# One hybrid decoder layer in fp32 on one core: two weight sums instead of three as side work, two sums formed in the second up phase, and the side work spread otherwise

## The chip, the cores and the metric

The kernel runs on one core of one Trainium2 chip. The metric is the device time of one execution in microseconds. The core's engines each run their own queue in order: TensorE (PE, with its weight loads PEld), VectorE (DVE), ScalarE (ACT), GpSimd (POOL) and SyncE (SP), which computes nothing and issues most DMAs. An instruction waits on semaphores of other engines or of DMAs; what is behind it in its queue waits with it.

## The reference

One decoder layer for 512 prompt tokens and 8 x 4 sample tokens, 544 columns in all. What matters here:

```python
z = rmsnorm(h, g) @ w_in            # pooling input, queries, six k/v sets, gates
A = pool_mixer(pool_in);  B = native_sparse_attention(q, kv)
h = h + rmsnorm((sig(ga) * (A @ w_pool_proj) + sig(gb) * (B @ w_nsa_proj)) @ w_out)
up = rmsnorm(h) @ w_up              # 2048 -> 2 * 5632, columns: val | gate
val, gate = split(up)
y = (gelu(causal_conv(gate)) * val) @ w_down
h = h + rmsnorm(y)
```

## The kernel before

Activations lie transposed: 128 channels on the partitions, 544 tokens along the free side, in two halves of 272. Every product in full fp32 accuracy is made of three: the high part of the weights by the high part of the activations, high by low, and low by high (L404 to L406). So each weight block is loaded raw and split.

**Units of weights.** `plan()` lists 1220 units in the order of use, most of four blocks of 128x128 (`UB`). The class `Weights` carries each through three steps. `load` issues the DMA into a raw tile `wr` (SP). `split` part 0 makes the high part `wh` on ScalarE (L247), part 1 the low part `wl` on VectorE (L249, raw minus high). `get` hands the unit to TensorE. `progress` is called between the matmuls of a unit: at a quarter and a half of it, it splits the unit that is `ahead` units further and issues a load beyond it. Raw tiles and parts come from rings of buffers that `grow` lengthens: three raw tiles in the opening, eight in the up phases.

**The up product.** It is a Winograd form of Strassen's scheme over halves of the contraction (k) and of the columns (val and gate) and the two token halves. For a column block j there are weight quarters 0 (gate, first k half), 1 (gate, second), 2 (val, first), 3 (val, second). The first up phase does quarters 0 and 1 with the first token half. The second up phase has per j five products, in this order: `t1` with weights s1 = q2 + q3, `t2` with s2 = s1 - q0, `b22` with s4 = q1 - s2, `t3` with s3 = q0 - q2, `t4` with q3. Two units make a product, ten units a column; 44 columns. `b22` adds into the bank of `t1` and `t3` into the bank of `t2`, so ScalarE's copy of `t1` (L1489, val) and VectorE's add from `t2` (L1491, sl) have to be done before. The conv of the column before (L1430 to L1441) runs beside it, in pieces that `later` issues.

**Side work.** s1, s2 and s3 are not known beforehand. `sum_stage` forms them during the input projections: for each of 88 pieces (j and half of k) it loads quarters 0, 2, 3 (`su`, 768 KB), does three VectorE operations in place (L367, L369, L371) and writes three sums back to DRAM (`sums_d`, 768 KB). The up phase loads them from there. s4 is formed when its unit is split: L246 subtracts the raw tile of s2, two units older, ahead of the cast. The su ring has three tiles, so the load of piece n + 2 waits for the write of piece n - 1.

**Order.** All of it is written out in one program order. `tick` is called between matmuls; it runs `later` calls that are due and steps two generators, `bg` (attention stages, residual chains, preparation) and `side` (the sums), each at a `rate`: a rate of 0.5 is a step for every second tick. `wait(n)` is n empty steps. The rates are set by hand at the stages (L1073 on). `h1_chain` (L1286 on) is the residual and norm chain of a token half; its squares are added up by GpSimd (L1309) and a matmul `nrh` (L428) sums them over the partitions.

In the opening, tokens arrive tile by tile (`x`, L475), ScalarE makes the high part (L479), VectorE the low (L480), ScalarE squares; units 0 to 15 each belong to one tile. There `ahead` is 1, from unit 14 on it is 2.

Of the kernel before, what the change touches and what calls it, by code (L numbers as in the profile page):

```python
# [12 lines left out]
F32 = mybir.dt.float32  # L13
# [3 lines left out]
OP = mybir.AluOpType  # L17
# [4 lines left out]
P = 128  # L22
# [12 lines left out]
FT = DFF // P  # L35
# [5 lines left out]
KH = KT // 2  # L41
UB = 4
UW = UB * P
# [60 lines left out]
def quad(j, q):  # L104


    if isinstance(q, str):
        b = [(q, k, j) for k in range(KH)]
    else:
        b = [("up", q % 2 * KH + k, (FT if q < 2 else 0) + j) for k in range(KH)]  # L110
    return [tuple(b[c:c + UB]) for c in range(0, KH, UB)]


SLOT = {"s2": 0, "s3": 1, "s1": 2}


def offsets(units):
# [61 lines left out]
class Weights:  # L179


    def __init__(self, nc, dram, sums, units):
        self.nc, self.dram, self.sums, self.units = nc, dram, sums, units
        self.i = self.nd = self.ns = 0
        self.raw, self.done = {}, {}
        self.rings = {"wraw": [], "wpart": []}
        self.turn = {"wraw": 0, "wpart": 0}
        self.ahead, self.raws = 1, 2
        self.off, _ = offsets(units)
        self.kept, self.again = {}, {}  # L190

# [16 lines left out]
    def load(self, n):  # L208
        while self.nd < min(n, len(self.units)):
            if self.nd in self.again:  # L210
                self.nd += 1
                continue
            i = self.nd
            pool, n_ = self.slot("wraw")
            t = self.raw[i] = pool.tile([P, UW], F32, name=f"wr{i}", tag="wraw", bufs=n_)
            b, w = self.units[i][0], self.width(i)
            mat, k, j = b[0]
            if mat in SLOT:
                src = self.sums[j, k // UB][:, SLOT[mat], :]
            else:  # L220
                o, n, q = self.off[quad(j, 1)[k // UB] if mat == "s4" else b]
                src = self.dram[o:o + n * P * w].rearrange("(p q c) -> p q c", q=n, c=w)[:, q, :]
            self.nc.sync.dma_start(t[:, :w], src)
            self.nd += 1

    def split(self, i, part):

        if i in self.again:
            if part == 0:
                self.done[i] = self.kept[self.again[i]]  # L230
            else:
                self.ns = i + 1
            return
        if part == 0:
            self.load(i + 1)
            if i in self.kept:
                self.done[i] = self.kept[i]
            else:
                pool, n = self.slot("wpart")
                self.done[i] = tuple(pool.tile([P, UW], F32R, name=f"w{p}{i}", tag="w" + p, bufs=n) for p in "hl")  # L240
        hi, lo = self.done[i]
        c = slice(0, self.width(i))
        raw = self.raw[i]
        if part == 0:
            if self.units[i][0][0][0] == "s4":
                self.nc.vector.tensor_tensor(raw, raw, self.raw[i - 2], OP.subtract)  # L246
            self.nc.scalar.copy(hi[:, c], raw[:, c])  # L247
        else:
            self.nc.vector.tensor_tensor(lo[:, c], raw[:, c], hi.bitcast(F32)[:, c], OP.subtract)  # L249
            self.raw.pop(i - 2, None)  # L250
            self.ns = i + 1

    def finish(self, i):
        while self.ns <= i:
# [25 lines left out]
def layer(ctx: ExitStack, tc: tile.TileContext, a: dict):  # L280
    nc = tc.nc
# [17 lines left out]
    dr, dr_es = pool("scratch", space=DRAM)  # L299
    psp, ps_es = pool("ps", space=PSUM)  # L300

    sums_d = dr.tile([FT, KH // UB, P, 3, UW], F32, name="sums_d")
    sup, su_es = pool("sums", "right")
    ws = Weights(nc, a["wst"], sums_d, plan())
    ws.grow(wp, 3, 3)
# [44 lines left out]
    def sum_stage():  # L350

        pieces = [(j, c) for j in range(FT) for c in range(KH // UB)]
        tiles = {}

        def load(n):
            j, c = pieces[n]
            t = tiles[n] = sup.tile([P, 3, UW], F32, name=f"su{j}_{c}", tag="su", bufs=3)
            o = ws.off[quad(j, 0)[c]][0]
            nc.sync.dma_start(t, a["wst"][o:o + 3 * P * UW].rearrange("(p q c) -> p q c", q=3, c=UW))

        load(0)
        load(1)
        yield from wait(10)
        for n, (j, c) in enumerate(pieces):
            t = tiles.pop(n)
            a11, a21, a22 = [t[:, q, :] for q in range(3)]
            V.tensor_tensor(a22, a21, a22, OP.add)  # L367
            yield
            V.tensor_tensor(a21, a11, a21, OP.subtract)  # L369
            yield  # L370
            V.tensor_tensor(a11, a22, a11, OP.subtract)  # L371
            yield from wait(2)
            if n + 2 < len(pieces):
                load(n + 2)
            yield from wait(4)
            nc.sync.dma_start(sums_d[j, c], t)
            yield from wait(2)

    def wait(n):
        for _ in range(n):  # L380
            yield
# [129 lines left out]
    for k in range(0, KT, 2):  # L511
        if k + 2 < KT:
            load_x(k + 2)
            load_x(k + 3)
        ws.load(k + 4)
        if k == 8:
            load_consts()
        if k == 0:
            ws.finish(0)
            split_x(1)  # L520
            square_x(0)
            square_x(1)
        if k + 2 < KT:
            split_x(k + 2)
            split_x(k + 3)
            square_x(k + 2)
            square_x(k + 3)
        if k == KT - 2:
            ws.ahead, ws.raws = 2, 3
            ws.finish(k + 2)  # L530
            for h in range(2):
                later(4 * h, lambda h=h: norm_factor([acc[:, HS[h]]], r1[:, HS[h]], f"nra{h}", (tmpn, tmps)))
            tick(0)
        for _ in range(2):
            unit(lambda mat, m: psA[m], U, lambda k: k == 0, lambda k: k == KT - 1, byk=True)
# [539 lines left out]
    def background():  # L1075
        yield from compress_stage()
        yield from natural_stage()
        t1_es.close()
        side["rate"] = 0.55
        yield from sample_stage()  # L1080
        s2_es.close()
        side["rate"] = 0.8
        yield from prompt_stage()

    bg["gen"] = background()
    bg["rate"] = 0.7
    side["gen"], side["rate"] = sum_stage(), 0.77

    first_evac()
    for m in range(3, 21):  # L1090
# [190 lines left out]
    def h1_chain(h):  # L1281

        sl = HS[h]
        xr, sq = {}, {}

        def load(k):  # L1286
            xr[k] = hp_.tile([P, H2], F32, name=f"xr{h}_{k}", tag="xr", bufs=4)
            nc.sync.dma_start(xr[k], a["xT"][:, k, sl])

        for k in range(3):  # L1290
            load(k)
        yield from wait(4)
        norm_factor([acc2[:, sl]], rm[:, sl], f"nrm{h}")
        yield
        for k in range(KT + 2):
            if k < KT:
                if k + 3 < KT:
                    load(k + 3)
                t = mo[:, k, sl]
                V.scalar_tensor_tensor(t, t, gains[:, 1, k:k + 1], rm[:, sl], OP.mult, OP.mult)  # L1300
                V.tensor_tensor(t, t, xr.pop(k), OP.add)
            if 1 <= k <= KT:
                j = k - 1
                t = mo[:, j, sl]
                sq[j] = acc3[:, sl] if j == 0 else hp_.tile([P, H2], F32, name=f"sqh{h}_{j}", tag="sqh", bufs=3)
                S.activation(sq[j], t, AF.Square)
                nc.sync.dma_start(h1_d[:, j, sl], t)
            if k > 2:
                G.tensor_tensor(acc3[:, sl], acc3[:, sl], sq.pop(k - 2), OP.add)  # L1309
            yield  # L1310
        yield from wait(5)
        norm_factor([acc3[:, sl]], r2[:, sl], f"nrh{h}")
        yield
        for k in range(KT + 1):
            if k < KT:
                t = mo[:, k, sl]
                V.scalar_tensor_tensor(t, t, gains[:, 2, k:k + 1], r2[:, sl], OP.mult, OP.mult)
            if h == 0:
                if k < KT:
                    S.copy(vh0[:, k, :], t)  # L1320
                if k:
                    V.tensor_tensor(vl0[:, k - 1, :], mo[:, k - 1, sl], vh0.bitcast(F32)[:, k - 1, :], OP.subtract)
            yield
# [48 lines left out]
    for h in range(2):  # L1372
        for m in range(KT - NSPLIT, KT):
            ps = bank(f"wo{m}_{h}", m, h)
            full("out", m, ps, MX, lambda m, h: mo_evac(m, ps, h))
        if h == 0:
            bg["gen"], bg["rate"], bg["credit"] = h1_chain(0), 0.85, 1.0
    drain()
    mg_es.close()
    w2p, w2_es = pool("weights2", "left")  # L1380
# [26 lines left out]
                    nc.sync.dma_start(stash_d[j + i], st[i])  # L1407
    drain()
    v0_es.close()
    gw, gw_es = pool("gate", "right")  # L1410
    cw, ch, co = ffn["cw"], ffn["ch"], ffn["co"]
    ge, stash = {}, {}
# [138 lines left out]
    for ci, (c0, c1) in enumerate(CHUNKS):  # L1551
# [21 lines left out]
        for n in range(ws.ahead, KT):  # L1573
            i = ws.i + n
# [29 lines left out]
    ad_es.close()  # L1604
    y_es.close()
    w2_es.close()
    w1_es.close()
    ps_es.close()
    dr_es.close()
# [94 lines left out]
```

## Time and profile before

| | |
|---|---|
| median of 3 runs | 3075.03 us (3069.4 to 3075.3) |
| profiled execution | 3070.8 us, span 3068.9 us, granted clock 0.98 |
| PE busy | 2914.3 us, 95% |
| DVE busy | 1888.4 us, 62% |
| ACT busy | 1149.4 us, 37% |
| moved by DMA | 593.04 MB, mean 193 GB/s |
| sum pieces loaded / written | 88 x 768 KB, 5.3 us to landing / 88 x 768 KB, 6.0 us |

The stages, by the trace: opening to about 62 us, input projections with the attention stages beside them to 956, pooling projection and mixer to 1124, the two projections and merge to 1322, output projection to 1538, first up phase to 1800, second to 2489, down product to the end. A busy PE is not PE at its peak, as matmuls are pipelined; idle time in front of an instruction and what ended it tell more. In a time line the start is in us from the span's start.

### The profile page before, as it was taken

Reading aid. Unit: us, or ns where it says so; the run is one execution under the profiler, and the core shown is the slowest. Engines: PE = TensorE matmul, PEld = TensorE weight load, DVE = VectorE, ACT = ScalarE, POOL = GpSimd, SP = SyncE. Lnnn points to the kernel's source line nnn. Section 1 sums busy time; section 2 is a strip of 40 time slices with the busy share of each in tenths; the row PEclk is TensorE's granted clock in tenths of the full one; section 3 lists DMA queues with packets and bytes.
Section 4 is the critical chain, followed back from the end, with each engine's and each line's share of the span. In section 5 each row is a group of like instructions: output and inputs, shape, how many; then the busy total and the mean of one; then the engine's idle time right before and its main releaser. Section 6 shows DMA issues by size and latency. Waiting matters only on the chain. (4 is left out here: it accounts for less than half of the span.)

```text
span 3068.9 us, 59917 instructions
## 1 busy us (share of the span) xinstructions
PE 2914.3 (95%) x22799; PEld 2805.6 (91%) x22799; DVE 1888.4 (62%) x3706; ACT 1149.4 (37%) x2390; POOL 258.1 (8%) x400
## 2 busy tenths in 40 slices
PE   7798898999999899999899999999999999999995
PEld 7788876899999799999899999999999999999995
DVE  5334443688886566644887557777777764444457
ACT  4111122444443132223456555555455453222223
POOL 3222221000000210001220000000000000000004
PEclk9899999999999999999999999999999999999998
DMA  4966677644555788844686666666666663333343
GB/s 152 249 226 231 226 262 268 218 156 164 180 182 180 197 260 294 293 128 122 179 277 218 229 218 205 206 204 202 203 204 205 212 203 114 111 110 109 100 130 105
DMA packets 304111, 593.04 MB, mean 193 GB/s; under 512 B 52811, under 2 KB 93164, under 8 KB 303822
## 3 DMA queue, kind: packets, MB, share of 16 engines
q1 hardware_dynamic: 280040, 557.74, 56.0%
q10 hardware_dynamic: 16614, 14.68, 2.1%
q0 software_dynamic: 7168, 16.79, 1.7%
q8 instruction: 179, 2.93, 0.4%
q14 instruction: 110, 0.90, 0.1%
HBM read 461.77 MB, written 127.31 MB: 192 GB/s over the span
## 5 line engine op out<-in xcount | busy, mean ns | idle before, releaser
L249 DVE TENSOR_TENSOR wl<-wr,wh 128x512 fp32r<-128x512 f32 (+1 forms) x1198 | 839.2, 707 | 782.8 <-ACT wh L247 671.7
L247 ACT CAST wh<-wr 128x512 fp32r<-128x512 f32 (+1 forms) x1198 | 726.8, 618 | 1278.7 <-PE dn L405 324.5
L404 PE MATMUL in<-uh,wh 128*128 128x272 f32 x1600 | 496.5, 310 | 42.2 <-DVE gz L1101 16.2
L406 PE MATMUL in<-uh,wl 128*128 128x272 f32 x1600 | 465.7, 291 | 2.5 <-DVE wl L249 2.5
L405 PE MATMUL in<-ul,wh 128*128 128x272 f32 x1600 | 465.6, 291 | 0.0
L404 PEld LDWEIGHTS in<-uh,wh 128*128 128x128 f32 x1600 | 305.8, 191 | 86.1 <-issue 73.7
L404 PE MATMUL dn<-h,wh 128*128 128x272 f32 x1320 | 380.6, 288 | 1.8 <-DVE y L1582 1.8
L406 PE MATMUL dn<-h,wl 128*128 128x272 f32 x1320 | 382.1, 289 | 0.0
L405 PE MATMUL dn<-l,wh 128*128 128x272 f32 x1320 | 379.7, 288 | 0.0
L406 PEld LDWEIGHTS in<-uh,wl 128*128 128x128 f32 x1600 | 305.6, 191 | 3.2 <-DVE wl L249 3.2
L405 PEld LDWEIGHTS in<-ul,wh 128*128 128x128 f32 x1600 | 306.8, 192 | 0.7
L404 PEld LDWEIGHTS dn<-h,wh 128*128 128x128 f32 x1320 | 249.0, 189 | 2.4 <-issue 2.4
L405 PEld LDWEIGHTS dn<-l,wh 128*128 128x128 f32 x1320 | 248.9, 189 | 0.0
L406 PEld LDWEIGHTS dn<-h,wl 128*128 128x128 f32 x1320 | 248.3, 188 | 0.0
L404 PE MATMUL p<-vh,wh 128*128 128x272 f32 x704 | 204.2, 290 | 0.1
L405 PE MATMUL p<-vl,wh 128*128 128x272 f32 x704 | 203.9, 290 | 0.0
L406 PE MATMUL p<-vh,wl 128*128 128x272 f32 x704 | 203.3, 289 | 0.0
L406 PE MATMUL wo<-mh,wl 128*128 128x272 f32 x512 | 150.9, 295 | 4.9 <-DVE wl L249 4.9
L404 PE MATMUL wo<-mh,wh 128*128 128x272 f32 x512 | 150.5, 294 | 2.0 <-ACT wh L247 1.9
L405 PE MATMUL wo<-ml,wh 128*128 128x272 f32 x512 | 149.2, 291 | 0.0
L404 PEld LDWEIGHTS p<-vh,wh 128*128 128x128 f32 x704 | 132.7, 188 | 0.4 <-ACT st L1405 0.3
L406 PEld LDWEIGHTS p<-vh,wl 128*128 128x128 f32 x704 | 132.5, 188 | 0.2 <-DVE wl L249 0.2
(353 smaller groups left out, 6854.6 us busy)
## 6 DMA issues: line engine op xcount, KB each, us to landing
wr<-wst SPq DMA_DIRECT2D x929, 256.0 KB, 3.4
su<-wst SPq DMA_DIRECT2D x88, 768.0 KB, 5.3
sums_d<-su SPq DMA_DIRECT2D x88, 768.0 KB, 6.0
wr<-sums_d SPq DMA_DIRECT2D x264, 256.0 KB, 3.1
stash_d<-st SPq DMA_DIRECT2D x44, 272.0 KB, 2.1
act_d<-val SPq DMA_DIRECT2D x44, 272.0 KB, 2.1
ar<-act_d SPq DMA_DIRECT2D x44, 272.0 KB, 3.0
sg_d<-gz SPq DMA_DIRECT2D x32, 272.0 KB, 2.1
```

The source lines that it names most:

```text
L247: self.nc.scalar.copy(hi[:, c], raw[:, c])
L249: self.nc.vector.tensor_tensor(lo[:, c], raw[:, c], hi.bitcast(F32)[:, c], OP.subtract)
L404: T.matmul(ps, wh, xh, start=first(k), stop=False, skip_group_check=skip)
L405: T.matmul(ps, wh, xl, start=False, stop=False, skip_group_check=skip)
L406: T.matmul(ps, wl, xh, start=False, stop=last(k), skip_group_check=skip)
```

## The change

- s3 is no longer formed as side work. `sum_stage` does two VectorE operations (s1, s2) and writes 512 KB a piece; it still loads three quarters. s3 is formed as q3 - s2 in the second up phase, from a plain load of quarter 3 and the raw tile of s2, four units older.
- Both subtracts (s4 and s3) move: `combine` issues them behind the low part of the unit before, not in front of the own cast. Two more raw buffers (`weights3`) hold the older tiles.
- The side work's rates: 0.35, 0.3, 0.85 and then 1.1, before 0.77, 0.55, 0.8.
- In the opening, units are split two ahead from the start, unit 1 before the loop.
- `h1_chain` waits 10 steps, not 5, ahead of its second norm; for the first half its rate is 1.0, not 0.85.

```diff
-SLOT = {"s2": 0, "s3": 1, "s1": 2}
+SLOT = {"s2": 0, "s1": 1}
+PLAIN = {"s4": 1, "s3": 3}
...
-        self.ahead, self.raws = 1, 2
+        self.ahead, self.raws = 2, 3
...
         if part == 0:
-            if self.units[i][0][0][0] == "s4":
-                self.nc.vector.tensor_tensor(raw, raw, self.raw[i - 2], OP.subtract)
             self.nc.scalar.copy(hi[:, c], raw[:, c])
         else:
             self.nc.vector.tensor_tensor(lo[:, c], raw[:, c], hi.bitcast(F32)[:, c], OP.subtract)
-            self.raw.pop(i - 2, None)
+            self.raw.pop(i - 4, None)
             self.ns = i + 1
+            self.combine(i + 1)
+
+    def combine(self, i):
+
+        mat = self.units[i][0][0][0] if i < len(self.units) else None
+        if mat in PLAIN:
+            self.nc.vector.tensor_tensor(self.raw[i], self.raw[i], self.raw[i - (2 if mat == "s4" else 4)], OP.subtract)
...
-        yield from wait(10)
+        yield from wait(12)
...
-            V.tensor_tensor(a22, a21, a22, OP.add)
-            yield
-            V.tensor_tensor(a21, a11, a21, OP.subtract)
-            yield
-            V.tensor_tensor(a11, a22, a11, OP.subtract)
+            V.tensor_tensor(a21, a21, a22, OP.add)
+            yield
+            V.tensor_tensor(a11, a21, a11, OP.subtract)
+            yield
...
-            nc.sync.dma_start(sums_d[j, c], t)
+            nc.sync.dma_start(sums_d[j, c], t[:, :2, :])
...
             ws.finish(0)
             split_x(1)
+            ws.finish(1)
...
-        side["rate"] = 0.55
+        side["rate"] = 0.3
...
-        side["rate"] = 0.8
+        side["rate"] = 0.85
         yield from prompt_stage()
+        side["rate"] = 1.1
...
-    side["gen"], side["rate"] = sum_stage(), 0.77
+    side["gen"], side["rate"] = sum_stage(), 0.35
...
-        yield from wait(5)
+        yield from wait(10)
         norm_factor([acc3[:, sl]], r2[:, sl], f"nrh{h}")
...
-            bg["gen"], bg["rate"], bg["credit"] = h1_chain(0), 0.85, 1.0
+            bg["gen"], bg["rate"], bg["credit"] = h1_chain(0), 1.0, 1.0
...
+    w3p, w3_es = pool("weights3", "right")
+    ws.grow(w3p, 2, 0)
```

**VectorE in the second up phase**, from column 30 into column 31 (units 898 to 907 are column 31; `wl903<-wr903,wh903` is the low part of unit 903, `cv30` the conv of column 30, `sl31` the add that reads the bank of `t2`). Before:

```order
L1503 TENSOR_TENSOR val30_28743<-sl30_28695,utr30_28742 128x272
L246 TENSOR_TENSOR wr903_28838<-wr903_28838,wr901_28798 128x512
L249 TENSOR_TENSOR wl903_28957<-wr903_28838,wh903_28956 128x512
L1435 SCALAR_TENSOR_TENSOR cv30_28948<-ge30_28697,cw_21334,cv30_28948 128x560
L1436 SCALAR_TENSOR_TENSOR cv30_28948<-ge30_28697,cw_21334,cv30_28948 128x560
L249 TENSOR_TENSOR wl904_28982<-wr904_28856,wh904_28981 128x512
L249 TENSOR_TENSOR wl905_29001<-wr905_28876,wh905_29000 128x512
L1440 TENSOR_TENSOR val30_28743<-val30_28743,cv30_28948 128x512
L1441 TENSOR_TENSOR val30_28743<-val30_28743,cv30_28948 128x32
L249 TENSOR_TENSOR wl906_29022<-wr906_28894,wh906_29021 128x512
L1491 TENSOR_TENSOR sl31_28904<-sl31_28904,ug31_28949 128x272
```

Now, from the same operation on (the subtract of unit 903 stands one row above the first):

```order
L1511 TENSOR_TENSOR val30_28719<-sl30_28670,utr30_28718 128x272
L248 TENSOR_TENSOR wl903_28935<-wr903_28815,wh903_28934 128x512
L257 TENSOR_TENSOR wr904_28833<-wr904_28833,wr900_28756 128x512
L1443 SCALAR_TENSOR_TENSOR cv30_28926<-ge30_28672,cw_21365,cv30_28926 128x560
L1444 SCALAR_TENSOR_TENSOR cv30_28926<-ge30_28672,cw_21365,cv30_28926 128x560
L248 TENSOR_TENSOR wl904_28960<-wr904_28833,wh904_28959 128x512
L257 TENSOR_TENSOR wr905_28853<-wr905_28853,wr901_28775 128x512
L248 TENSOR_TENSOR wl905_28980<-wr905_28853,wh905_28979 128x512
L1448 TENSOR_TENSOR val30_28719<-val30_28719,cv30_28926 128x512
L1449 TENSOR_TENSOR val30_28719<-val30_28719,cv30_28926 128x32
L248 TENSOR_TENSOR wl906_29001<-wr906_28871,wh906_29000 128x512
L1499 TENSOR_TENSOR sl31_28881<-sl31_28881,ug31_28927 128x272
```

The s4 subtract of unit 903 went above the add into val30, and the two s3 subtracts (units 904 and 905) stand ahead of the conv and between the low parts of 904 and 905. ScalarE's order there is the same as before; its cast of 905 now has that subtract in front of it.

**SP after the opening**, from the first sum pieces on (`su0_0` is the load of a piece, `wr20` that of unit 20). Before:

```order
L359 DMA su0_0_1046<-wst 128x1536
L359 DMA su0_1_1048<-wst 128x1536
L223 DMA wr20_1054<-wst 128x512
L548 DMA kvT<-cz_114 128x544 x3
L223 DMA wr21_1087<-wst 128x512
L223 DMA wr22_1117<-wst 128x512
L223 DMA wr23_1147<-wst 128x512
L223 DMA wr24_1184<-wst 128x512
L359 DMA su1_0_1195<-wst 128x1536
L548 DMA kvT<-cz_114 128x544
L223 DMA wr25_1217<-wst 128x512
L376 DMA sums_d_71<-su0_0_1046 128x1536
```

Now:

```order
L224 DMA wr20_1050<-wst 128x512
L365 DMA su0_0_1058<-wst 128x1536
L365 DMA su0_1_1060<-wst 128x1536
L553 DMA kvT<-cz_114 128x544 x3
L224 DMA wr21_1087<-wst 128x512
L224 DMA wr22_1117<-wst 128x512
L224 DMA wr23_1147<-wst 128x512
L224 DMA wr24_1181<-wst 128x512
L553 DMA kvT<-cz_114 128x544
L224 DMA wr25_1212<-wst 128x512
L224 DMA wr26_1249<-wst 128x512
L224 DMA wr27_1280<-wst 128x512
```

The third piece load and the first write-back have left this place; they come behind units 31 and 34.

**SP in the two projections** (units 286 to 292). Before:

```order
L223 DMA wr286_15114<-wst 128x512
L223 DMA wr287_15146<-wst 128x512
L359 DMA su40_1_15174<-wst 128x1536
L223 DMA wr288_15183<-wst 128x512
L223 DMA wr289_15213<-wst 128x512
L376 DMA sums_d_71<-su39_1_14945 128x1536
L223 DMA wr290_15256<-wst 128x512
L359 DMA su41_0_15284<-wst 128x1536
L223 DMA wr291_15290<-wst 128x512
L223 DMA wr292_15324<-wst 128x512
```

Now:

```order
L224 DMA wr286_15007<-wst 128x512
L365 DMA su37_1_15018<-wst 128x1536
L224 DMA wr287_15039<-wst 128x512
L381 DMA sums_d_71<-su36_1_14858 128x1024
L224 DMA wr288_15075<-wst 128x512
L365 DMA su38_0_15093<-wst 128x1536
L224 DMA wr289_15108<-wst 128x512
L381 DMA sums_d_71<-su37_0_14936 128x1024
L224 DMA wr290_15150<-wst 128x512
L365 DMA su38_1_15178<-wst 128x1536
L224 DMA wr291_15184<-wst 128x512
L381 DMA sums_d_71<-su37_1_15018 128x1024
```

A piece now stands to every two units here, before to every three. In SP's order up to the load of unit 134 (four ahead of unit 130) there are 16 piece loads and 14 write-backs, before 32 and 30; from there to that of unit 212, 27 and 26, before 25 and 25; behind it 45 and 48, before 31 and 33. Both finish ahead of the output projection.

In the opening, the loads of `x4` and `x5` stand behind those of units 4 and 5; before they stood ahead of unit 4. The low part of unit 1 stands ahead of the low parts of `x2` and `x3` on VectorE, before behind them.

## Rows read from the trace of the kernel before

**Rows 1.** Busy time by stage: start:end, length, engines (instructions), clock, DMA share, GB/s.

```profile
62.00:135.00 73.00, 52.72 (x373) 50.34 (x371) 29.40 (x53) 10.98 (x18) 16.92 (x34) 0.86 0.87 230
135.00:570.00 435.00, 396.47 (x3169) 348.34 (x3169) 181.46 (x478) 88.11 (x183) 94.56 (x172) 0.96 0.72 243
956.00:1124.00 168.00, 150.18 (x1113) 144.91 (x1112) 90.10 (x166) 38.61 (x69) 31.30 (x28) 0.95 0.73 206
1124.00:1322.00 198.00, 194.78 (x1535) 193.74 (x1534) 130.14 (x228) 55.13 (x95) 0.00 (x0) 0.99 0.83 285
1830.00:2440.00 610.00, 602.17 (x4693) 593.43 (x4693) 468.44 (x861) 306.07 (x627) 3.89 (x39) 1.00 0.63 205
...
1140.00:1150.00 10.00, 10.00 (x82) 10.00 (x81) 9.01 (x18) 3.07 (x5) 0.00 (x0) 1.00 0.92 335
```

**Rows 2.** Waits of PE over the span: releaser, us in total, times, longest.

```profile
PE cps L666 <- DMA X<-cache: 17.7, 3, 7.8
PE in L404 <- DVE gz L1101: 16.2, 7, 7.2
PE in L404 <- DVE kz L555: 15.6, 1, 15.6
PE st L404 <- ACT wh L247: 11.2, 6, 2.7
PE uqk L404 <- ACT val L1489: 10.7, 43, 2.4
PE po L404 <- ACT wh L247: 9.2, 4, 4.1
...
PE nrh L428 <- POOL acc L1309: 4.6, 1, 4.6
```

**Rows 3.** Waits of SP's queue from 62 to 570.

```profile
SPq L359 <- DMA sums_d<-su: 35.8, 10, 11.6
```

**Rows 4.** Waits of SP's queue from 956 to 1322.

```profile
SPq L359 <- DMA sums_d<-su: 62.2, 18, 6.6
```

**Rows 5.** Time line of DVE, one column: start, duration, operation [idle before, releaser].

```profile
2148.20 0.44 DVE L1498 TENSOR_TENSOR sl<-sl,ug 128x272 f32<-128x272 f32 x1 [0.29 <-PE ug L406]
...
2151.08 0.69 DVE L249 TENSOR_TENSOR wl<-wr,wh 128x512 fp32r<-128x512 f32 x1 [0.76 <-PE utr L405]
...
2152.03 0.69 DVE L246 TENSOR_TENSOR wr<-wr,wr 128x512 f32<-128x512 f32 x1
...
2154.24 0.81 DVE L1435 SCALAR_TENSOR_TENSOR cv<-ge,cw,cv 128x560 f32<-128x560 f32 x1
...
2157.13 1.50 DVE L249 TENSOR_TENSOR wl<-wr,wh 128x512 fp32r<-128x512 f32 x2 [1.25 <-PE ug L405]
2158.55 0.69 DVE L1440 TENSOR_TENSOR val<-val,cv 128x512 f32<-128x512 f32 x1
...
2159.25 0.69 DVE L249 TENSOR_TENSOR wl<-wr,wh 128x512 fp32r<-128x512 f32 x1
2159.85 0.43 DVE L1491 TENSOR_TENSOR sl<-sl,ug 128x272 f32<-128x272 f32 x1
...
2163.79 0.44 DVE L1498 TENSOR_TENSOR sl<-sl,ug 128x272 f32<-128x272 f32 x1 [0.29 <-PE ug L406]
```

**Rows 6.** Time line of ACT, the same column.

```profile
2152.83 0.62 ACT L247 CAST wh<-wr 128x512 fp32r<-128x512 f32 x1 [1.78 <-DVE wr L246]
2153.36 0.85 ACT L1430 ACTIVATE cv<-ge,cw 128x560 f32<-128x560 f32 x1
...
2156.50 0.60 ACT L247 CAST wh<-wr 128x512 fp32r<-128x512 f32 x1
2157.01 0.38 ACT L1489 COPY val<-uqk 128x272 f32<-128x272 f32 x1
2157.28 1.66 ACT L247 CAST wh<-wr 128x512 fp32r<-128x512 f32 x3
```

**Rows 7.** Time line of PE, the same column.

```profile
2157.44 0.39 PE L404 MATMUL uqk<-b22h,wh 128*128 128x272 f32 x1 [0.20 <-ACT val L1489]
...
2160.57 0.29 PE L404 MATMUL ug<-t3h,wh 128*128 128x272 f32 x1
```

More of the change, by code (lines that the diff above doesn't have):

```diff
@@ L220, in load @@
             else:
-                o, n, q = self.off[quad(j, 1)[k // UB] if mat == "s4" else b]
+                o, n, q = self.off[quad(j, PLAIN[mat])[k // UB] if mat in PLAIN else b]
                 src = self.dram[o:o + n * P * w].rearrange("(p q c) -> p q c", q=n, c=w)[:, q, :]
@@ L300, in layer @@
     psp, ps_es = pool("ps", space=PSUM)
-    sums_d = dr.tile([FT, KH // UB, P, 3, UW], F32, name="sums_d")
+    sums_d = dr.tile([FT, KH // UB, P, 2, UW], F32, name="sums_d")
     sup, su_es = pool("sums", "right")
@@ L528, in layer @@
         if k == KT - 2:
-            ws.ahead, ws.raws = 2, 3
             ws.finish(k + 2)
@@ L1606, in layer @@
     w2_es.close()
+    w3_es.close()
     w1_es.close()
```

## The prediction

> **What bounds the kernel now.** I read the stages first, then who TensorE waits for, then one column of the stage that the new subtract goes into. TensorE is the bound: it is busy 602.2 of 610 us in the steady part of the second up phase [rows 1]. Its losses lie early: 20.3 us idle in the 73 us from 62 to 135, 38.5 us in the 435 us up to 570, 17.8 us in the pool stage from 956 to 1124 [rows 1]. By cause, the largest waits are 17.7 us for the page loads of the compression, 16.2 us behind VectorE in the gate evacuations, 15.6 us once in the kv evacuation, and 11.2 us for weight casts in the opening [rows 2]. The single wait of 15.6 us belongs to the sum work: SP, whose queue carries every weight load, stood up to 11.6 us at the load of a sum piece until an older piece was written back [rows 3].
>
> In the second up phase nothing looks late in that list except 10.7 us (43 waits) for the copy of val [rows 2]. The reader is to see there that one column's VectorE and ScalarE work is a single chain. It begins when the t3 product ends (L1498 at 2148.20) and it returns 15.59 us later (2163.79) [rows 5]. Two of its links hold TensorE: the copy of val (2157.01, ends 2157.39) frees the b22 product at 2157.44, and L1491 (2159.85, ends 2160.28) reads the bank that the t3 product adds to from 2160.57 [rows 5 to 7]. The second has only 0.29 us to spare.
>
> **The change, part by part.** *The third weight sum in the second up phase.* One VectorE subtract of 128x512 leaves each of the 88 sum pieces; 88 new ones stand in the second up phase, two a column, and every subtract there (L257) stands behind the low part of the unit before. I follow the column of rows 5 to 7 in the new order, with these steps of the old: a subtract's start to its cast's start 0.80 us (2152.03 to 2152.83); a cast's start to its low part's start 0.63 (2156.50 to 2157.13); VectorE's spacing of two such operations 0.60 (2159.25 to 2159.85).
> The low part of the first s4 unit starts at 2151.08 as before. The second s4 subtract follows it at 2151.68 (it stood at 2152.03). Its cast comes at 2152.48, the conv's first step on ScalarE 0.53 us later at 2153.01 and, lasting 0.85, ready at 2153.86. But VectorE now does the low part at 2153.11 and the new s3 subtract at 2153.71, so L1435's successor starts at 2154.31, against 2154.24. The gain of 0.35 us is eaten, and the val copy is 0.07 us later.
> From there: the next cast at 2156.57, its low part at 2157.20, the second s3 subtract at 2157.80, and only then its cast, at 2158.60; that low part at 2159.23 (before: 2157.91, from a cast at 2157.28 that waited for no subtract); L1440's successor at 2159.83, the next low part 0.70 us later at 2160.53, L1491's successor at 2161.13, ended after 0.43 at 2161.56. TensorE may start t3 some 0.05 us after that, at 2161.61 instead of 2160.57: 1.04 us late. A restart costs about 0.1 more (the first matmul behind the val wait took 0.39 against 0.29 [rows 7]). A column has no slack to win this back, since the chain starts again from the end of t3. 44 columns x 1.15 us = 51 us. Bounds: nothing, if the bank's reader were not waited for, and 60 us, if each of the two subtracts delayed the whole column by 0.69. I take +51, since the same steps explain the old column: from its cast at 2157.28 they put L1491 at 2159.81, where it is at 2159.85 [rows 5, 6].
>
> The row of that stage shows VectorE busy 468.4 of 610 us, 77% [rows 1]; two more subtracts of 0.69 us in 15.59 make 86%, still under TensorE. The Trainium skill (Perfetto Trace Analysis, Identifying the Most-Contended Engine) judges VectorE's headroom by just this occupancy. By it the subtracts would cost nothing and the sum would be 51 us lower, as in the first rival; the trace here agrees that VectorE has room, and not that the room lies where the column could use it.
>
> *The sum work thinned early.* By the order, the part up to unit 130 (to 570 us) keeps 16 piece loads of 32 and 14 write-backs of 30, and a write-back is 512 KB instead of 768. Of the 16.8 MB moved from 62 to 135 (230 GB/s) some 4.7 MB leave, three loads and three writes of 0.79. No load of a piece stands in SP's way there any more, so the 11.6 us go, while the rest of the traffic, that kept the DMA engines 87% busy, stays. Bounds 0 and -16; I take -10. The waits for the page loads: 32 loads a group are issued one after another and the last one's landing is waited for; less traffic shortens landings, not the number of issues. Bounds 0 and -18; I take half, -9. The gate waits (16.2): SP is held there by the sample's own loads and stores as well; bounds 0 and -16, I take -8. The clock returns some with each: 0.86 granted from 62 to 135 and 0.96 to 570 [rows 1]; that is at most another 10 us, which I leave to the range.
>
> *The sum work packed later.* From unit 208 to the drain 45 loads stand where 31 stood. In the pool stage SP already waits for write-backs, 62.2 us in 18 waits up to 1322 [rows 4], and TensorE for casts behind it, 9.2 us [rows 2]. Between the write-back of a tile and its next load there are now one or two weight loads, before two or three. More waits of that kind, less bytes in each: bounds -6 and +18, I take +4. In the projections behind it the 285 GB/s over 198 us [rows 1] become 63 MB, 319 GB/s. TensorE was busy all of a stretch at 335 [rows 1], so the bytes fit; what SP's order costs is bounded by 0 and +20, I take +3.
>
> *The opening.* Units 1 and 2 are split earlier, which takes waits of 2 us; but x4 and x5 now stand in SP's queue behind two weight loads that wait for the low parts of units 1 and 2, and from then on each pair of x loads waits for a split as before. Every cast of a later unit stands behind those x tiles on ScalarE. Bounds -8 and +8 (of 11.2 us [rows 2]); I take +3.
>
> *The residual chain of the first half.* The norm matmul nrh keeps its place in TensorE's order; its adds are issued at rate 1.0 instead of 0.85, so they end earlier. The wait was 4.6 us [rows 2]; a denser VectorE there may delay low parts. Bounds -8 and +4, I take -3. The longer wait ahead of the second norm and the two more raw buffers cost nothing: nothing waits for the second norm before the first up phase is over, and the buffers only keep the operands of the new subtract alive.
>
> Sum: +51 -10 -9 -8 +4 +3 +3 -3 = +31 us. The profiled execution took 3070.8 us, between the lowest run and the median (3075.0); set against their middle, 3073, that gives **3104 us**.
>
> **The rivals.** 1. *The subtracts hide.* For it: VectorE's 77%, and its idle stretches in the column, 0.76 us ahead of 2151.08 and 1.25 us ahead of 2157.13 [rows 5]. Against it: each of those idle stretches is a wait for ScalarE inside the chain, and the second s3 subtract makes a new one. The sum without the 51 us is -20: 3053 us, faster. It decides from the point where L1491's successor ends within 0.29 us of its old place in the column.
> 2. *The early stalls go altogether.* The three groups give 49 us and the clock up to 10 us instead of 27: 3104 - 32 = 3072 us, about no change. For it: all three stand behind SP or a landing. Against it: the page loads' issues and the sample stage's own transfers stay.
> 3. *The late packing overloads SP's queue.* The pool stage and the projections lose their upper bounds, 38 us instead of 7: 3135 us. For it: the 62.2 us of SP waits and the shorter way from write-back to load. Against it: a write-back is a third smaller.
>
> **How the numbers follow.** Forecast 0.60, rival 1 0.17, rival 2 0.12, rival 3 0.11. The forecast's own range is 3085 to 3122. The whole range reaches down to rival 1 and up to rival 3: 3050 to 3136. A measurement tells 0.2%, 6 us, from no change. Faster: rival 1 and 0.05 of rival 2, 0.22. Within: 0.06 from rival 2. Slower: the rest, 0.72.
>
> **What would show it.** Right: in the second up phase a column of about 16.7 us, a wait of the first t3 matmul for the add into sl of about a microsecond, 44 times, and two subtracts of s3 in VectorE's rows; the wait of 15.6 us gone; the piece loads' waits on write-backs less before 570 us and not less from 956 on. Wrong: columns of 15.6 us, or a t3 matmul that waits for nothing; then the chain has slack that I did not see, and the change is faster by what it saves early.

## The result, and the profile after

The changed kernel takes 3161.1 us (median), the kernel before 3073.4: a ratio of 1.0282, with a 95% interval from 1.0261 to 1.0302. It is slower, as forecast, but by 88 us where 31 were predicted, and outside the range that ended at 3136. One of its four runs took 4174.7 us at a granted clock of 0.61, where the others show 0.98, and is left out of the ratio.

The two profiled executions span 3068.9 and 3154.1 us. Cut where each stage's first cast starts, the 85 us between them come about like this (us; the stages left out differ by less than 1.5):

| stage | before | after | difference | predicted |
|---|---|---|---|---|
| opening (units 0 to 15) | 61.6 | 64.7 | +3 | +3 |
| input projections up to unit 130 | 507.7 | 488.8 | -19 | -27 |
| gates to unit 208 | 386.9 | 387.3 | 0 | 0 |
| pool stage | 167.7 | 182.3 | +15 | +4 |
| the two projections | 198.4 | 231.6 | +33 | +3 |
| output projection, last part | 98.7 | 100.2 | +1.5 | -3 |
| second up phase | 689.4 | 741.4 | +52 | +51 |

The busy times by stage, of the changed kernel (start:end, length, then PE, PEld, DVE, ACT, POOL busy with their counts, PE's granted clock, DMA share, GB/s), each stretch cut at its own stage:

```profile
64.70:134.80 70.10, 50.33 (x342) 47.76 (x343) 25.54 (x46) 10.80 (x18) 18.62 (x36) 0.85 0.76 181
134.80:553.50 418.70, 400.94 (x3199) 351.55 (x3199) 148.61 (x423) 88.01 (x183) 94.56 (x172) 0.98 0.60 194
940.80:1123.10 182.30, 154.42 (x1119) 148.90 (x1119) 90.79 (x162) 38.20 (x69) 30.58 (x28) 0.93 0.77 203
1123.10:1354.70 231.60, 208.90 (x1548) 200.55 (x1548) 130.25 (x229) 56.06 (x96) 0.00 (x0) 0.98 0.85 274
1870.00:2480.00 610.00, 569.28 (x4365) 553.25 (x4364) 475.04 (x873) 281.94 (x580) 3.63 (x36) 1.00 0.57 192
```

Against [rows 1], TensorE is now idle for 41 us of 610 in the second up phase, where it was idle for 8, and VectorE's busy time has hardly moved (475 against 468): two subtracts more a column, but longer columns. In the projections the DMA engines move less per second than before (274 GB/s against 285) and TensorE waits all the same.

Who TensorE waits for, over the span of the changed kernel (releaser, us in total, times, longest):

```profile
PE ug L409 <- DVE sl L1499: 35.3, 42, 0.8
PE uqk L409 <- ACT val L1497: 15.8, 43, 3.6
PE po L409 <- ACT wh L246: 13.7, 5, 6.1
PE in L409 <- DVE gz L1107: 12.8, 9, 4.1
PE in L409 <- DVE kz L560: 12.8, 1, 12.8
PE np L409 <- ACT wh L246: 9.7, 9, 1.8
...
PE pp L409 <- ACT wh L246: 6.6, 5, 2.2
...
PE nra L433 <- POOL acc L493: 4.8, 1, 4.8
...
PE cps L671 <- DMA X<-cache: 3.4, 2, 3.2
```

The first row is new: the `t3` product waits for the add into `sl` once a column. The waits for the page loads have nearly gone (17.7 to 3.4 us), the gate waits a little (16.2 to 12.8), and the single wait for `kz`, which was to lose 10 us, lost 2.8 [rows 2]. In the projections the casts are late again and again.

One column of the second up phase, first VectorE, then ScalarE and TensorE (start, duration, operation, idle before and its releaser):

```profile
2199.41 0.69 DVE L248 TENSOR_TENSOR wl<-wr,wh 128x512 fp32r<-128x512 f32 x1 [1.25 <-ACT wh L246]
2200.02 0.68 DVE L257 TENSOR_TENSOR wr<-wr,wr 128x512 f32<-128x512 f32 x1
2201.44 0.69 DVE L248 TENSOR_TENSOR wl<-wr,wh 128x512 fp32r<-128x512 f32 x1 [0.74 <-ACT wh L246]
2202.05 0.69 DVE L1448 TENSOR_TENSOR val<-val,cv 128x512 f32<-128x512 f32 x1
...
2203.36 0.43 DVE L1499 TENSOR_TENSOR sl<-sl,ug 128x272 f32<-128x272 f32 x1
...
2216.21 0.69 DVE L248 TENSOR_TENSOR wl<-wr,wh 128x512 fp32r<-128x512 f32 x1 [1.25 <-ACT wh L246]
```

```profile
2200.79 2.78 ACT L246 CAST wh<-wr 128x512 fp32r<-128x512 f32 x5 [1.13 <-DVE wr L257]
```

```profile
2199.71 0.40 PE L409 MATMUL uqk<-b22h,wh 128*128 128x272 f32 x1 [0.29 <-ACT val L1497]
...
2203.84 0.39 PE L409 MATMUL ug<-t3h,wh 128*128 128x272 f32 x1 [0.85 <-DVE sl L1499]
```

A column now takes 16.80 us (2199.41 to 2216.21). The reader is to see the detour: the second s3 subtract (2200.02) starts only when the low part of the first s3 unit is done, ScalarE waits 1.13 us for it, VectorE then 0.74 us for that cast, and the add into `sl` follows 3.95 us after the first low part, where it took 2.72 [rows 5]. TensorE stands 0.85 us for it.

And SP's queue, its waits from 940 to 1123 us, and from 1123 to 1355 us:

```profile
SPq L365 <- DMA sums_d<-su: 69.2, 12, 7.7
...
SPq L365 <- DMA sums_d<-su: 137.0, 27, 8.7
```

Before, in the same two stages:

```profile
SPq L359 <- DMA sums_d<-su: 24.4, 6, 6.6
...
SPq L359 <- DMA sums_d<-su: 37.8, 12, 6.4
```

It stood 62.2 us in 18 waits over both stages before [rows 4], now 206 us in 39. One turn of the ring in the projections, from one piece load to the next:

```profile
1236.90 0.33 SPq L365 DMA_DIRECT2D su<-wst  x1
1237.33 0.37 SPq L224 DMA_DIRECT2D wr<-wst  x1
1237.75 0.42 SPq L381 DMA_DIRECT2D sums_d<-su  x1
1239.01 0.33 SPq L224 DMA_DIRECT2D wr<-wst  x1
1245.74 0.33 SPq L365 DMA_DIRECT2D su<-wst  x1
```

The piece load at 1245.74 waits until the write-back issued at 1237.75 has landed, 8 us later. In this turn of 8.8 us SP issues two weight loads, one of them behind the write-back; at the pace of before (198.4 us for the 64 units of the projections) TensorE uses up two units in some 6 us.

### The profile page after: what moved, and what is told of

Same layout as the page of the kernel before. It is cut to its first block, busy times and chain, and to the rows that moved or that the text cites. A ratio compares the mean times of both kernels' runs of the same rounds, so it can differ in the third digit from the quotient of the medians.

```text
span 3154.1 us, 59952 instructions
## 1 busy us (share of the span) xinstructions
PE 2945.6 (93%) x22799; PEld 2815.5 (89%) x22799; DVE 1884.6 (60%) x3706; ACT 1148.4 (36%) x2390; POOL 256.3 (8%) x400
## 4 chain that ended last, share of the span: by engine, by line
PE 54%; DVE 13%; DMA 10%; issue 5%; ACT 4%; SPq 1%; ACTq 0%; DVEq 0%; POOL 0%; POOLq 0%
PE dn L411 5%; PE dn L409 5%; PE dn L410 5%; DMA sums_d<-su 4%; DMA wr<-wst 4%; DVE wl L248 4%; PE in L409 4%; ACT wh L246 3%; PE in L410 3%; PE in L411 3%; PE p L409 3%; PE p L410 3%; PE p L411 3%; DVE wr L257 3%; PE ug L409 2%
## 5 line engine op out<-in xcount | busy, mean ns | idle before, releaser
L409 PE MATMUL in<-uh,wh 128*128 128x272 f32 x1600 | 495.6, 310 | 34.9 <-DVE gz L1107 12.8
L409 PE MATMUL ug<-t3h,wh 128*128 128x272 f32 x352 | 106.1, 301 | 35.4 <-DVE sl L1499 35.3
```

The source lines that it names most:

```text
L409: T.matmul(ps, wh, xh, start=first(k), stop=False, skip_group_check=skip)
```

## The experiments

All medians stand against the kernel before, run beside them on the same chip (3073 to 3078 us); the ratios come with their 95% intervals.

**The subtract in front of the low part.** Only the place of the subtract is changed, in `split`:

```diff
+            self.combine(i + 1)
             self.nc.vector.tensor_tensor(lo[:, c], raw[:, c], hi.bitcast(F32)[:, c], OP.subtract)
             self.raw.pop(i - 4, None)
             self.ns = i + 1
-            self.combine(i + 1)
```

> The changed kernel with one thing turned round: a subtract of s4 or s3 is issued in front of the low part of the unit before, not behind it. Every instruction stays, VectorE's work is the same. Theory (the chain): the second s3 subtract then runs in the 1.25 us in which VectorE waits ahead of the first s3 unit's low part, the cast of the second s3 unit no longer waits for it, and the add into sl is ready in time. The column goes from 16.80 us to 15.6 or less; by the steps of the rows it would be bound by TensorE alone, about 15.1. Second up phase 53 to 73 us shorter, time 3088 to 3108. Rival (VectorE's occupancy, two more subtracts a column): the column stays at 16.8 and the time within 10 us of 3161.

It took 3081.7 us, 1.0033 [1.0019, 1.0047] of the kernel before: 79 us less than the changed kernel, and better than the 3088 to 3108 that were expected. Busy time in the same 610 us, and VectorE's rows of one column:

```profile
1870.00:2480.00 610.00, 610.00 (x4839) 610.00 (x4838) 528.21 (x968) 320.08 (x649) 3.98 (x40) 1.00 0.63 212
```

```profile
2199.99 0.44 DVE L1506 TENSOR_TENSOR sl<-sl,ug 128x272 f32<-128x272 f32 x1 [0.30 <-PE ug L411]
...
2206.34 0.68 DVE L257 TENSOR_TENSOR wr<-wr,wr 128x512 f32<-128x512 f32 x1
2207.66 1.50 DVE L249 TENSOR_TENSOR wl<-wr,wh 128x512 fp32r<-128x512 f32 x2 [0.65 <-ACT wh L246]
...
2215.12 0.44 DVE L1506 TENSOR_TENSOR sl<-sl,ug 128x272 f32<-128x272 f32 x1 [0.29 <-PE ug L411]
```

The column is 15.13 us, TensorE never waits in it, and VectorE is busier than ever (528 of 610 us, 87%). The subtract at 2206.34 fills a wait that was there anyway. The second up phase takes 666.8 us, 75 less than in the changed kernel and 23 less than before. So the 52 us were the place of the subtracts against the low parts, and neither the subtracts themselves nor VectorE's load. The occupancy rival falls. The edit moves all four subtracts of a column; that the second s3 subtract makes the detour is read from the rows above, not tried alone.

**The piece load four steps later.**

```diff
-            yield from wait(2)
+            yield from wait(6)
             if n + 2 < len(pieces):
                 load(n + 2)
-            yield from wait(4)
             nc.sync.dma_start(sums_d[j, c], t[:, :2, :])
```

> The changed kernel with the load of piece n + 2 moved four steps later, to just ahead of the write-back of piece n, so that 10 steps instead of 6 lie between the write-back of piece n - 1 and the load that reuses its tile. Bytes, rates and counts of DMAs are the same. Theory (SP's queue): the 48 us lost between 940 and 1355 us come from SP standing at piece loads (206 us in 39 waits there, mean 5.3) with weight loads behind them; four steps at rate 1.1 are about 2.8 us, so the waits shrink to 90 us or less and the two stages by 25 to 45 us: 3116 to 3136. Rival (bytes): the DMA engines are 80 to 85% busy there, more than before; the transfers stay late and the time stays within 8 us of 3161.

3140.1 us, 1.023 [1.021, 1.025]: 21 us less than the changed kernel, outside both expectations. SP's waits in the pool stage and in the projections, and the busy times of the projections:

```profile
SPq L365 <- DMA sums_d<-su: 36.0, 9, 6.9
...
SPq L365 <- DMA sums_d<-su: 74.2, 25, 5.9
```

```profile
1120.30:1340.40 220.10, 203.63 (x1545) 196.68 (x1543) 129.85 (x229) 55.52 (x97) 0.00 (x0) 0.99 0.88 288
```

The stand went from 206 to 110 us. The projections went from 231.6 to 220.1, but the pool stage stayed (183.6, from 182.3), although the stand there went from 69 to 36 us. SP's stand is a part of the loss in the projections; how large, this run leaves open. For the pool stage it shows no gain from a shorter stand.

**The last piece loads from GpSimd.**

```diff
-            nc.sync.dma_start(t, a["wst"]...
+            (G if n >= 61 else nc.sync).dma_start(t, a["wst"]...
```

> The changed kernel with the last 27 piece loads (those of the two projections, from 1123 us on) issued from GpSimd, which computes nothing there, instead of SP. Bytes, rates and the ring of three tiles stay; but a load that waits for a write-back no longer has weight loads behind it. Theory (SP's queue): the two projections, 231.6 us in the changed kernel, come down to 200 to 208 us, the time to 3130 to 3138. Rival (bytes, at 274 GB/s with the DMA engines 85% busy): they stay at 225 or more and the time at 3153 to 3165. The late load, which halved SP's stand and gave 11 us there, leaves both open; between 208 and 225 each has a share.

3129.2 us, 1.0178 [1.0164, 1.0192]. The projections:

```profile
1121.00:1328.50 207.50, 199.76 (x1541) 195.65 (x1540) 129.46 (x229) 54.81 (x97) 14.30 (x27) 0.99 0.88 306
```

```profile
SPq L224 <- DVE wl L248: 113.9, 43, 5.9
```

They took 207.5 us, 24 less, with the same pieces at the same rate; the bytes now go at 306 GB/s. SP stands for the low parts again, as it does when its weight loads are early (113.9 us; 24.2 in the changed kernel, 96.0 before), and no longer for write-backs. So 24 of the 33 us lost there came from piece loads in SP's queue, with weight loads behind them. One thing else changed with it: the moved loads travel in another DMA queue (q0 moves 38.0 MB, 16.8 in the changed kernel). This run does not part the two; that the late load gave 11.5 us here with every piece load still in SP's queue shows that the stand is a good part. The Trainium skill (DMA: Bandwidth & Descriptors, Issuing engines are not separate DMA queues) says that issuing DMAs from several engines saves only the sequencer's time to initiate them, usually little. Here it saved 24 us, where an issue takes some 0.4 us of SP's time: the wait for the older write-back stands on the issuing engine too. The other 9 us (207.5 against the 198.4 of before) were not taken apart.

**The rates of before.** `side["rate"]` is 0.77, 0.55, 0.8, 0.8 for 0.35, 0.3, 0.85, 1.1; all else as changed.

> The changed kernel with the side work's four rates as before (0.77, 0.55, 0.8, 0.8), all else as changed. Theory (late packing costs, thinning early gains): the stages from 940 to 1355 us go back to the lengths of before, 366 us instead of 414, or a little less, since a write-back is a third smaller; the stages up to 570 us give back 10 to 18 us. Time 3161 - 48 + 14 = 3127, 3115 to 3135. Rival (the early stages got shorter for the smaller write-backs, not for the rates): the early gain stays and the time is 3113 or less. Second rival (late stages are slow for another reason than the rate, such as two weight loads between write-back and load): 3161 to 3175.

3105.9 us, 1.0116 [1.0097, 1.0135]. Pool stage and projections:

```profile
942.30:1102.80 160.50, 149.02 (x1125) 144.65 (x1124) 81.21 (x151) 38.32 (x68) 30.89 (x28) 0.96 0.74 196
1102.80:1295.20 192.40, 191.43 (x1523) 190.77 (x1523) 118.62 (x209) 55.39 (x97) 0.00 (x0) 1.00 0.80 266
```

Together 352.9 us, 61 less than with the changed rates and 13 less than before. The profiled execution is the fastest of the five (3096.2); `first_old` below, with the same rates and the same code up to there, has 166.5 and 193.0 us, together 359.5, so 54 to 61 us less. The first part up to unit 130 stayed short: 494.5 us (497.0 in `first_old`), against 507.7 before and 488.8 with the changed rates. So more than half of the early gain belongs to what this kernel shares with the changed one, of which the smaller write-backs are the likeliest part (not tried alone), and the thinning itself gave some 6 to 8 us. The theory on the late stages holds; on the early ones the rival does, and the time is the rival's too.

**The strips apart.** The four writes of `strip_d` with `wait(7)` instead of `wait(3)` between them.

> The changed kernel with the four writes of strip_d (768 KB each in rows of some 1.5 KB, from ScalarE's queue) seven steps apart instead of three. The wait of 12.8 us ahead of the fifth in product's second group is still there after the change, though no sum piece stands in SP's way; in its stretch the DMA engines are 99% busy at 100 to 130 GB/s, 61% of their time with these four writes. Theory (the strips): the weight load that ends that wait lands earlier, and the wait shrinks by 6 us or more; the time is 3150 to 3156. Rival (SP's order: raw tiles are free too late): the wait stays within 2 us of 12.8 and the time within 5 us of 3161.

3142.7 us, 1.0245 [1.0222, 1.0268], 18 us less than the changed kernel and more than was expected. The DMA engines from 110 to 132 us of the changed kernel (busy tenths and GB/s in 40 slices; queue, packets, MB, share of the 16 engines; the issues), SP's row of three weight loads in it, and TensorE's wait in this run:

```profile
DMA  9889999999899899999899898999899998999999
GB/s 95 100 176 264 351 398 337 268 174 101 100 112 110 100 119 118 129 131 123 96 95 95 93 107 104 121 144 154 169 239 235 201 257 204 214 241 207 202 186 156
...
q10 hardware_dynamic: 1328, 1.97, 74.0%
q1 hardware_dynamic: 679, 1.26, 15.5%
...
strip_d<-sb ACTq DMA_DIRECT2D x2, 768.0 KB
wr<-wst SPq DMA_DIRECT2D x3, 256.0 KB
```

```profile
111.79 12.89 SPq L224 DMA_DIRECT2D wr<-wst  x3
```

```profile
PE in L409 <- DVE kz L560: 6.0, 1, 6.0
```

The wait halved. The queue q10, whose packets of 1.5 KB are the rows of the strip writes, holds 74% of the engines' time (all queues together 96%; the 99% of the expectation was too high), and the weight load that all wait for shares the rest. SP's three issues of weight loads take 12.9 us there, 4.3 us each, where one takes some 0.4 in the turn shown above. The sum pieces, which I had charged with this wait, were not its main cause. The wait is 6.8 us of the 18: the input projections up to unit 130 are 12 us shorter in all, and what gave the rest was not taken apart.

**Both mends together, and with the strips.** The first kernel joins the turned subtract and the old rates; the second adds `wait(7)`.

> Both mends together: the subtracts in front of the low part of the unit before, and the side work's rates as before (0.77, 0.55, 0.8, 0.8). If the two losses are independent (the column's chain and the late packing), their gains add up: 3106 less the 79 us that the turned order gave is 3027, 3020 to 3034, faster than the kernel before by 1.3 to 1.7%. Rival (what is gained early in a column is limited by the weight loads, or the sums' end): above 3040.

3034.0 us, 0.9867 [0.9847, 0.9887], at the upper end of what was expected: the two mends add up, within 7 us.

> Both mends, and the strip_d writes seven steps apart. With the kernel before it the strips run tells whether the 18 us that it gave belong to the early stages alone: theory 3027 - 14 = 3013, 3008 to 3020; if it gains only where the early rates are low, 3022 to 3030.

3028.0 us, 0.9853 [0.983, 0.9875], in the range of the second expectation; the interval overlaps that of the kernel without `wait(7)`. The `kz` wait fell from 15.2 to 9.3 us, but a wait of 7.3 us for `vz` and one of 9.7 for `gz` came up, so at the old rates moving the strips apart mostly moved the wait.

**The turned subtract in the kernel before.** Three sums stay side work.

```diff
-            if self.units[i][0][0][0] == "s4":
-                self.nc.vector.tensor_tensor(raw, raw, self.raw[i - 2], OP.subtract)
...
+            if i + 1 < len(self.units) and self.units[i + 1][0][0][0] == "s4":
+                self.nc.vector.tensor_tensor(self.raw[i + 1], self.raw[i + 1], self.raw[i - 1], OP.subtract)
             self.nc.vector.tensor_tensor(lo[:, c], raw[:, c], hi.bitcast(F32)[:, c], OP.subtract)
```

> The kernel before (three sums as side work, its rates) with one edit: the s4 subtract is issued in front of the low part of the unit before instead of ahead of its own cast. It tells what the new place of the subtract is worth without the third sum in the second up phase. Theory: the column of before, 15.59 us, was held by the same chain, and loses its 0.45 us: 15.13, 20 us over 44 columns, time 3050 to 3056. Rival (the 15.1 of the turned order comes from s3 being formed late, from plain quarters): the column stays at 15.6, the time at 3073.

3050.2 us, 0.9927 [0.9907, 0.9946], the column 15.13 us, the second up phase 666.3. The kernel before already lost 23 us in this chain. `first_old`, with all else of the change at the old rates, is 16 us faster still. By the profiles the stages that hold the side work gain some 20 us (10 of them up to unit 130, 9 in the pool stage and the projections) with two sums instead of three, and the new opening and the residual chain at rate 1.0 give back 4; the third sum's move was not tried without these two.

**Tuning what is left.** `spread` adds the strips apart, the late piece load and rates 0.6, 0.5, 1.15, 0.65 to the turned subtract; the next two undo one part of the change each (`h1_chain(0)` at 0.85; splits one ahead in the opening); `best` joins these with a last rate of 0.72.

> Both mends, the strips apart, the piece load just ahead of the write-back, and rates 0.6, 0.5, 1.15, 0.65: by the order 26 piece loads up to unit 134, 35 to unit 212 (27 in the changed kernel, 25 before) and 27 behind it (46 and 32). Theory: between units 134 and 212 TensorE waits for almost nothing and the DMA engines are half busy, so pieces cost nothing there; the pool stage and the projections get a few us shorter, to some 345 us. Time 3000 to 3012. Rival (VectorE, 80% busy in the prompt stage, or SP standing at the loads there): that stage (387 us) gets longer by more than the others gain; over 3015.

3025.3 us, 0.9838 [0.9816, 0.986]: the time is the rival's, its reason is not. The gates stayed at 387.9 us with 35 pieces, so pieces are free there, and the pool stage took 154.8 us, against 166.5 in `first_old`; but the projections took 199.1 us, with pieces left for their end, against 193.0, although SP stood only 2.3 us there for write-backs.

> The kernel with both mends, the strips apart and the pieces spread, with one thing of the change undone: the first half's residual chain at rate 0.85 instead of 1.0. The last part of the output projection took 98.7 us before and 100.2 with the change; the wait for nrh (4.6 us) is gone, but 14 us of waits for casts and low parts of wo stand there. Theory (the denser chain delays the splits by as much as it wins): the part goes to 98.5 to 99, the time to 3022 to 3025, within what can be measured. Rival (the casts wait for something else): 100.2 stays, or with the nrh wait back up to 105.

3024.2 us, 0.9834 [0.9815, 0.9852]. The last part of the output projection took 96.0 us instead of 100.2, less than expected, without the nrh wait coming back; in the total this is inside the interval.

> The same kernel with the opening of before: splits one ahead until the last pair of tiles, unit 1 not split ahead of the loop. The changed opening took 56.7 to 61.1 us in seven profiles, that of before 56.8 and 57.0 in two. Theory (the new opening costs 2 us and a wait of 3 to 5 us of the first norm): the time goes down by 2 to 5 us, to 3020 to 3023. Rival (it gains, and the difference comes from the DMAs' timing): 3025 to 3033.

3020.3 us, 0.982 [0.9807, 0.9833]. The direction is that of the theory, the intervals overlap.

> The spread kernel with the opening of before, the residual chain's rate of 0.85 and a last side rate of 0.72 instead of 0.65: by the order the last piece is loaded at unit 307 instead of 317, so that none is left for the end of the projections. The opening gave 5 us and the chain's rate 1 us by the medians; the last part of the projections (112.2 us with the spread, 106.5 with the old rates) should give 4 to 6. If they add up: 3025 - 5 - 1 - 5 = 3014, 3009 to 3019. Rival (the gains are one and the same DMA slack): 3019 to 3025.

3024.2 us, 0.983 [0.9814, 0.9845]. The rival: the small gains did not add up. These four kernels can't be told from each other; all are 1.6 to 1.8% faster than the kernel before.

## Why the prediction was wrong

*The column* was right. The chain of steps gave 16.74 us and a `t3` start 1.04 us late; measured are 16.80 us and a wait of 0.85, in the place that the text named, 42 times. +51 us predicted, +52 measured. The two parts of the 1.15 us were off and balanced: against [rows 1], TensorE is idle 0.92 us more in a column and busy 0.29 us more, where 1.04 and 0.1 were put down. That the chain and not VectorE's 77% decides was shown by the turned subtract: at 87% TensorE waits for nothing. What I missed is how cheap the way out was: the 1.25 us of idle time that I counted as part of the chain take a subtract that is issued ahead of the waiting low part. (I called this idle time a wait for ScalarE; [rows 5] name TensorE as its releaser. The cast ahead of it ended only 0.03 us before [rows 6], and in the changed kernel the same 1.25 us are put to the cast.)

*The sum work packed later* is the term that failed: +4 and +3 us, with bounds of +18 and +20, measured +15 and +33. Of the 57 us between 3104 and 3161 these are 41, and the early gains another 8. Its step was "the bytes fit; what SP's order costs is bounded by 0 and +20". The bytes did go faster, at 306 GB/s, once the piece loads had left SP's queue. The order was mis-sized, by reading only the count of weight loads between a write-back and the next load, and that count was misread: from 956 to 1322 us it was two before, or one (4 of 31 turns), not "two or three"; it is one in 29 of 46 turns now. The ring of three tiles ties each piece load to the write-back issued just before it, six steps earlier; a higher rate shortens these six steps in time, but not the landing of the write-back, so the wait per piece grows while the pieces come closer together. Before, 12 waits of 3.15 us were hidden by the split's lead in the projections, where TensorE waited 3.2 us in all; 27 waits of 5.1 us were not. This row was in the profile: with a median landing of 6 us, a turn of the ring can't be shorter than that plus what SP issues in it, and the rate of 1.1 asks for a turn in about two units, some 6 us. SP's queue is shown as the cause for 24 of the 33 us in the projections. The 15 us of the pool stage go with the rate (160.5 and 166.5 us at the old ones), but how the rate costs them is open, since halving the stand there changed nothing. Rival 3 had the mechanism, but I set it against the forecast as an alternative of 38 us, where the range ended; its price was 48.

*The sum work thinned early* gave 19 us of the 27. The page loads gained more than I took (14 us for 9), the gate waits less (3 for 8), and the `kz` wait 2.8 for 10: it hung on the strip writes, and my "No load of a piece stands in SP's way there any more, so the 11.6 us go" mistook a wait in SP's queue nearby for its cause. The rates themselves bought only some 6 to 8 us.

*The residual chain* was right on the wait and wrong on the sum: the 4.6 us at nrh went, and waits of 14 us for casts and low parts stand in that part (before 6.6), for +1.5 us; at rate 0.85 it took 96.0. *The opening* measured +3 as predicted, with some luck: ten profiles with this same opening lie between 56.7 and 61.1 us from the first cast on, four with that of before between 55.7 and 57.6, and the means are 1.8 us apart.

## What to carry to other kernels

On an engine that runs in order, issue work that is ready ahead of an instruction that will wait, not behind it: with the subtracts behind the low parts the second up phase took 741 us, with them in front of the low parts 667. Before a rate of side work is raised, set the ring's turn (write-back landing plus what its queue issues) against the time that the new rate leaves for it, and look at which queue stands in the meantime. And a wait found next to a long one is its cause only if the chain runs through it.

## What the runs showed of the hardware

With 27 loads issued from another engine a stage took 24 us less with unchanged bytes: SP no longer stood for their semaphores, and the loads travelled in another DMA queue; the run doesn't part the two. Writes in rows of 1.5 KB kept the DMA engines at eight tenths and more while all queues together moved 93 to 131 GB/s for some 9 us, against 306 GB/s over the projections in the run from GpSimd; beside these writes one issue of a weight load took SP 4.3 us instead of some 0.4. And TensorE ran 610 us without one wait beside a VectorE that was 87% busy.
